# Moving operands stored from the last column to the first, and the two parts of each weight stored as a pair

## The chip, the cores and the metric

The kernel runs on one core of a Trainium2 chip. The metric is the time on the device in microseconds (us), and a time of a kernel is the median of its runs. Five engines are named throughout: PE is TensorE (matrix products; PEld is its loading of weights, which it lists apart), DVE is VectorE, ACT is ScalarE, POOL is GpSimd, and SP is SyncE, which here only issues transfers from memory.

## The reference, cut to what matters

A decoder trunk of two layers works on 272 tokens (16 learned ones and 256 real ones) of 2048 numbers each, all in float32. Layer 0 is a short gated convolution, layer 1 is attention with a forget gate over shared keys and values; each is followed by a SwiGLU with 5632 hidden units.

```python
h = concatenate([meta, x])                                    # 272 tokens x 2048
h = h + short_conv_mixer(rms_norm(h, a_norm), a_w_in, a_conv, a_w_out)
h = h + swiglu(rms_norm(h, ffn_norm[0]), ffn_w_gu[0], ffn_w_down[0])
k, v, c = shared_kv(h, kv_norm, w_kv, k_norm, w_f, b_f)       # 16 heads of 128
h = h + forgetting_attention(rms_norm(h, b_norm), b_w_q, b_q_norm, b_w_o, k, v, c)
h = h + swiglu(rms_norm(h, ffn_norm[1]), ffn_w_gu[1], ffn_w_down[1])
return h[:, 16:, :]

def swiglu(xn, w_gu, w_down):
    g, u = split(xn @ w_gu, 2, axis=-1)
    return (silu(g) * u) @ w_down
```

Nearly all of the arithmetic is products of a weight matrix with the normed tokens, and every weight (415 MB in all) is used once for each token.

## The kernel before

**How a product is made.** Activations lie transposed, 128 model dimensions on the partitions and the tokens along the free axis. A product of weights w and tokens x is made from a high and a low part of each (tiles of type fp32r): w_high x_high + w_high x_low + w_low x_high. `mm3` (lines 105 to 108) issues these three matmuls for one 128x128 block of weights, each over all tokens: 272 columns, or 256 where only the real tokens count. In layer 1's SwiGLU the two parts of x, 256 columns each, lie side by side and fit one accumulator, so that `product` (lines 110 to 121) takes both in a single matmul of 512 columns (L118 for the first, L121 for the others) and w_low x_high in one of 256 (L119). PE takes the block of weights in a load of its own (PEld) ahead of each matmul; x is the moving operand that streams past it. There are 17,126 PE instructions in the program besides loads.

**The stream of weights.** `add_panel` (line 66) cuts all weights into panels of 1 MB. SP loads them one after the other into three buffers (`RAW_BUFS`, lines 76 to 87). Each panel is two half panels, which `split` (lines 89 to 103) divides: ScalarE copies a half panel of 128 partitions x 1024 weights into the high part `whi` (L99), VectorE subtracts it from the weights and writes the low part `wlo` (L100). There are 784 half panels and four buffers for each part (`SPLIT_BUFS`). The loop at the end of the kernel (lines 774 to 781) emits the matmuls of half panel i, then the split of half panel i+3, then the steps due after i (`post` and `hooks`: gates, norms, residual adds, attention). `add_up4`, `add_up` and `add_down` (lines 123 to 204) say which blocks of weights meet which tiles of x and into which accumulator: a half panel is 24 matmuls of `mm3`, or 16 of `product`.

**The moving operands.** They are of three kinds. `make_operand` (line 231) makes the 16 tiles `x0` to `x15` of a normed input: one tile of 544 columns with the high part first and the low part behind it (L237 and L238). `put_hidden` (line 282) does the same for the tiles of the second product of a stage, in `hid` (L285, L286). `make_xb` (line 425) makes the input of the query product, in two tiles `bh` and `bl`.

**What sets the order.** The kernel is written in Tile's framework, which inserts the semaphores and sets the order of each engine's queue by a simulated timeline. Within a queue an engine works strictly in that order.

Of the kernel before, what the change touches and what calls it, by code (L numbers as in the profile page):

```python
# [10 lines left out]
F32R = mybir.dt.float32r  # L11
# [4 lines left out]
P = 128  # L16
NM = 16            # meta tokens
S = 256            # real tokens
T = NM + S         # all tokens
D = 2048  # L20
KT = D // P        # 16 tiles of the model dimension
F = 5632
FT = F // P        # 44 tiles of the hidden dimension
H = 16             # heads, each of 128
EPS = 1e-6
# [4 lines left out]

RAW_BUFS = 3       # weight panels in flight, 1 MB each
SPLIT_BUFS = 4     # half panels split into high and low parts


@with_exitstack
def kernel(ctx, tc, x, meta, a_norm, a_w_in, a_conv, a_w_out, kv_norm, w_kv,
# [15 lines left out]
    def nm(s):  # L52
        uid[0] += 1
        return f"{s}_{uid[0]}"
# [7 lines left out]

    # ---------------------------------------------------------------- weight stream
    panels, slabs, hooks = [], [], {}

    def add_panel(src, cut, mms, posts):
        """src: [128, a, b] view of 2048 elements a partition in DRAM; cut: a or b is halved."""
        j = len(panels)
        panels.append((src, cut))
        for s in range(2):  # L70
            slabs.append({"panel": j, "half": s, "mm": mms[s], "post": list(posts[s])})
        return len(slabs) - 2
# [16 lines left out]
    def split(i):  # L89
        if i >= len(slabs):  # L90
            return
        sl = slabs[i]
        j, s = sl["panel"], sl["half"]
        src, cut = panels[j]
        raw = raw_t[j].rearrange("p (a b) -> p a b", a=src.shape[1])
        part = raw[:, 4 * s:4 * s + 4, :] if cut == "a" else raw[:, :, 256 * s:256 * s + 256]
        hi = wpool.tile([P, 4, 256], F32R, tag="whi", name=nm("whi"), bufs=SPLIT_BUFS)
        lo = wpool.tile([P, 4, 256], F32R, tag="wlo", name=nm("wlo"), bufs=SPLIT_BUFS)
        A.activation(hi, part, AF.Copy)  # L99
        V.tensor_tensor(out=lo, in0=part, in1=hi.bitcast(F32), op=ALU.subtract)  # L100
        split_t[i] = (hi, lo)
        if s == 1:
            load(j + RAW_BUFS)

# [5 lines left out]
    def product(acc, cols, whi, wlo, x, first, last):  # L110
        """acc (+)= w^T x from the parts of both. With x's parts side by side the high part of w
        meets both in one instruction, and acc then holds two halves that add up."""
        xhi, xlo, both = x
        if both is None:
            mm3(acc[:, cols], whi, wlo, xhi, xlo, first, last)
        else:
            if first:
                PE.matmul(acc, whi, both, start=True, stop=False)  # L118
            PE.matmul(acc[:, S:2 * S], wlo, xhi, start=False, stop=False)  # L119
            if not first:  # L120
                PE.matmul(acc, whi, both, start=False, stop=last)  # L121

    def add_up4(w, col, xs, cols, post, delay=0):
        """Four output tiles w[:, col:col+512]^T x over all of the model dimension."""
        accs = {}
        for pnl in range(4):
            src = w[pnl * 512:(pnl + 1) * 512, col:col + 512].rearrange("(k p) c -> p k c", p=P)

            def mk(s, pnl=pnl):
                def mm(hi, lo):  # L130
                    xl = xs()
                    for m in range(2):
                        if pnl == 0:
                            accs[2 * s + m] = ps("acc")
                        for k in range(4):
                            product(accs[2 * s + m], cols, hi[:, k, m * P:(m + 1) * P],
                                    lo[:, k, m * P:(m + 1) * P], xl[4 * pnl + k],
                                    pnl == 0 and k == 0, pnl == 3 and k == 3)
                return mm

            i = add_panel(src, "b", [mk(0), mk(1)], [[], []])
        for s in range(2):
            done = lambda s=s: [post(m, accs[m]) for m in (2 * s, 2 * s + 1)]
            if delay:
                hook(i + s + delay, done)
            else:
                slabs[i + s]["post"].append(done)

    def add_up(w, col, xs, cols, post, delay=0):
        """Two output tiles w[:, col:col+256]^T x over all of the model dimension.  # L150
        post(m, acc) consumes each one."""
        accs = []
# [28 lines left out]
    def add_down(w, row, xs, cols, post, plain=16):  # L181
        """All of the 16 output tiles, with 4 tiles of the contraction from row on."""
        first = None
# [24 lines left out]

    # ---------------------------------------------------------------- constants
    ident = const.tile([P, P], F32, name="ident")  # L210
# [16 lines left out]

    # ---------------------------------------------------------------- normed operands
    state = {}

    def make_operand(key, src, gain, cols):
        """High and low parts of src * gain, for the tensor engine."""
        k = len(state[key])
        n = cols.stop - cols.start
        both = wt(f"x{k}", [P, 2 * T], F32R)
        hi, lo = both[:, 0:n], both[:, n:2 * n]
        A.activation(hi, src, AF.Copy, scale=gain)  # L237
        V.scalar_tensor_tensor(out=lo, in0=src, scalar=gain, in1=hi.bitcast(F32),  # L238
                               op0=ALU.mult, op1=ALU.subtract)
        state[key].append((hi, lo, both[:, 0:2 * n] if 2 * n <= 512 else None))  # L240

# [13 lines left out]
    def rsqrt_dve(out, m, y2):  # L255
        """out = m ** -0.5 on VectorE: a first guess from the exponent bits, then Newton."""
        V.tensor_scalar(out=out.bitcast(I32), in0=m.bitcast(I32), scalar1=-0.5,
# [18 lines left out]
    def new_hidden():  # L276
        return wt("hid", [P, 4, 2 * T], F32R, bufs=2)

    def hidden_parts(hid, k, n):
        return hid[:, k, 0:n], hid[:, k, n:2 * n]  # L280

    def put_hidden(hid, k, src, n):
        """src split into tile k of a chunk of the contraction."""
        hi, lo = hidden_parts(hid, k, n)
# [3 lines left out]
    def hidden_view(hid, n, both=False):  # L288
        return [hidden_parts(hid, k, n) + (hid[:, k, 0:2 * n] if both else None,) for k in range(4)]

# [19 lines left out]

    # ---------------------------------------------------------------- start: x to [d, token]
    start = tc.tile_pool(name="start", bufs=1)
# [56 lines left out]

    # ---------------------------------------------------------------- short convolution  # L370
    a_in, a_out = a_w_in[0], a_w_out[0]
# [53 lines left out]
    def make_xb(m):  # L425
        if m == 0:
            state["xb"] = []
        hi = wt(f"bh{m}", [P, S], F32R)
        lo = wt(f"bl{m}", [P, S], F32R)
        t = wt("bias", [P, P + NM + T], bufs=2)[:, 0:S]  # L430
# [5 lines left out]

    # ---------------------------------------------------------------- SwiGLU
    def ffn_phase(layer, cols, after):
# [48 lines left out]

    # ---------------------------------------------------------------- attention
    cdram = dram.tile([H, T], F32, name="cdram")
# [37 lines left out]
    heads = {}  # L527
    # columns of the two query blocks side by side: the first sees 144 keys, the second all
    QW = (slice(0, P + NM), slice(P + NM, P + NM + T))

    def head_square(d, name, raw, n):
        """High and low parts of the squares, for the sum over the head's 128 rows."""
        sq = wt("sq", [P, T], bufs=3)[:, 0:n]
# [7 lines left out]
    def head_norm(d, name, gain, n, tag):  # L541
        """raw * rsqrt(mean of squares + eps) * gain, split; on every partition the sums."""
        raw, sh, sl = d[name]
# [33 lines left out]

    # The keys: block A is 0:128, block B 144:272, which the first 128 queries never see, and
    # between them 16 keys whose parts are stacked on the partitions, all three products in one.
    KA, KC, KB = slice(0, P), slice(P, P + NM), slice(P + NM, T)  # L580

    def stack3(dst, src, order):
        """Tile of [high, high, low] or [high, low, high] parts of src, 16 columns each."""
        hi, again, lo = (dst[..., c:c + NM] for c in order)
# [150 lines left out]

    # ---------------------------------------------------------------- end: back to [token, d]
    fin = {}
# [23 lines left out]

    # ---------------------------------------------------------------- emission
    start_loads()
# [47 lines left out]
```

## Time and profile before

| | |
|---|---|
| time, median of 3 runs (lowest to highest) | 2381.14 us (2380.77 to 2381.97) |
| span of the profiled execution | 2376.3 us |
| PE busy | 2368.8 us, 100%, 17,266 matmuls |
| PEld busy | 2267.5 us, 95% |
| VectorE, ScalarE, GpSimd busy | 67%, 49%, 21% |
| chain of work that ended last | 97% PE |
| read from memory | 415.70 MB, 176 GB/s |

The profile is one execution, so the rows below add up to its own span and not to the median of the runs. PE works through a queue in which matmuls overlap: one begins before the one ahead of it has left the array. The durations listed for single matmuls therefore add up to more than the span, and what a matmul costs is the distance from its start to the next one's. Two views give that: single instructions in order of time, and a table by stretches, in which a count of matmuls stands beside the length of the stretch. Where PE is busy without a gap, its rows of waits say whether another engine came too late anywhere.

### The profile page before, as it was taken

What the parts mean: (1) busy time and instruction counts of PE and PEld (TensorE: products, weight loads), DVE (VectorE), ACT (ScalarE), POOL (GpSimd) and SP (SyncE); (2) the same over time, 40 slices, a digit from 0 to 9 for tenths busy, and PEclk for the clock granted to TensorE, in tenths of its full rate; (3) what the DMA queues carried; (4) which work ended last, traced back from release to release, by engine and by line L of the source; (5) the groups of instructions that cost most, each with busy time, mean ns of one, the idle gap of its engine ahead of it and who ended that gap; (6) DMA issues with size and microseconds to landing.
All of it is one profiled execution on the core that took longest, in us unless ns stands there. A gap on an engine that the chain in (4) does not pass through costs nothing.

```text
span 2376.3 us, 42180 instructions
## 1 busy us (share of the span) xinstructions
PE 2368.8 (100%) x17266; PEld 2267.5 (95%) x17266; DVE 1600.8 (67%) x2350; ACT 1170.3 (49%) x1800; POOL 505.0 (21%) x585
## 2 busy tenths in 40 slices
PE   9999999999999999999999999999999999999999
PEld 8999999999999999999999999999888888888888
DVE  6665658566556566556688667678677677777677
ACT  5443345434334333433577565666555555555555
POOL 4110113000000000000155242423033223222234
PEclk9999999999999999999999999999999999999999
DMA  6555555555555555555555555545555555555554
GB/s 228 172 175 177 178 178 178 170 173 174 177 178 178 177 175 173 172 174 177 178 163 156 164 166 165 159 151 178 195 185 187 194 183 190 190 184 195 191 182 141
DMA packets 236674, 420.53 MB, mean 177 GB/s; under 512 B 6961, under 2 KB 59281, under 8 KB 236465
## 3 DMA queue, kind: packets, MB, share of 16 engines
q1 hardware_dynamic: 235408, 415.40, 53.1%
q8 instruction: 136, 2.23, 0.4%
q0 software_dynamic: 1072, 2.44, 0.4%
q14 instruction: 58, 0.47, 0.1%
HBM read 415.70 MB, written 2.11 MB: 176 GB/s over the span
## 4 chain that ended last, share of the span: by engine, by line
PE 97%; issue 1%; DMA 1%; DVE 0%; ACT 0%; POOL 0%; SPq 0%; POOLq 0%; ACTq 0%
PE acc L107 21%; PE acc L106 21%; PE acc L108 21%; PE acc L121 18%; PE acc L119 10%; PE acc L118 3%; DMA ck<-cdram 0%; PE aux L108 0%; PE aux L107 0%; PE aux L106 0%; DMA raw<-in_a_w_in_dram 0%; PE aux L656 0%; ACT whi L99 0%; DVE wlo L100 0%; PE aux L676 0%
## 5 line engine op out<-in xcount | busy, mean ns | idle before, releaser
L100 DVE TENSOR_TENSOR wlo<-raw,whi 128x1024 fp32r<-128x1024 f32 x784 | 1019.9, 1301 | 643.5 <-ACT whi L99 638.5
L99 ACT ACTIVATE whi<-raw 128x1024 fp32r<-128x1024 f32 x784 | 829.7, 1059 | 922.2 <-PE acc L107 708.0
L106 PE MATMUL acc<-x,whi 128*128 128x272 f32 x2688 | 778.5, 290 | 0.4 <-ACT whi L99 0.4
L108 PE MATMUL acc<-x,wlo 128*128 128x272 f32 x2688 | 775.4, 289 | 0.0
L107 PE MATMUL acc<-x,whi 128*128 128x272 f32 x2688 | 774.5, 288 | 0.0
L107 PEld LDWEIGHTS acc<-x,whi 128*128 128x128 f32 x2688 | 511.4, 190 | 0.1
L106 PEld LDWEIGHTS acc<-x,whi 128*128 128x128 f32 x2688 | 505.9, 188 | 2.0 <-ACT whi L99 0.8
L108 PEld LDWEIGHTS acc<-x,wlo 128*128 128x128 f32 x2688 | 505.2, 188 | 0.0
L121 PE MATMUL acc<-x,whi 128*128 128x512 f32 x1320 | 462.0, 391 | 0.0
L119 PE MATMUL acc<-x,wlo 128*128 128x256 f32 x1408 | 380.6, 280 | 0.0
L107 PE MATMUL acc<-hid,whi 128*128 128x272 f32 (+1 forms) x1224 | 352.0, 288 | 0.0
L108 PE MATMUL acc<-hid,wlo 128*128 128x272 f32 (+1 forms) x1224 | 351.1, 287 | 0.0
L106 PE MATMUL acc<-hid,whi 128*128 128x272 f32 (+1 forms) x1224 | 349.1, 286 | 0.0
L121 PEld LDWEIGHTS acc<-x,whi 128*128 128x128 f32 x1320 | 247.8, 188 | 51.0
L119 PEld LDWEIGHTS acc<-x,wlo 128*128 128x128 f32 x1408 | 264.4, 188 | 7.4
L108 PEld LDWEIGHTS acc<-hid,wlo 128*128 128x128 f32 x1224 | 230.8, 189 | 0.1
L106 PEld LDWEIGHTS acc<-hid,whi 128*128 128x128 f32 x1224 | 230.8, 189 | 0.0
L107 PEld LDWEIGHTS acc<-hid,whi 128*128 128x128 f32 x1224 | 230.6, 188 | 0.0
L459 POOL TENSOR_TENSOR cs<-cs,rstd 128x272 f32<-128x272 f32 (+1 forms) x44 | 33.3, 756 | 911.4 <-DVE cs L457 911.4
L306 POOL TENSOR_TENSOR h<-h,u 128x256 f32<-128x256 f32 x172 | 155.6, 931 | 258.8 <-DVE h L305 258.8
L121 PE MATMUL acc<-hid,whi 128*128 128x512 f32 x522 | 192.2, 398 | 0.0
L119 PE MATMUL acc<-hid,wlo 128*128 128x256 f32 x696 | 167.2, 280 | 0.0
(194 smaller groups left out, 2378.1 us busy)
## 6 DMA issues: line engine op xcount, KB each, us to landing
raw<-in_ffn_w_gu_dram SPq DMA_DIRECT2D x176, 1024.0 KB, 5.0
raw<-in_ffn_w_down_dram SPq DMA_DIRECT2D x88, 1024.0 KB, 5.0
raw<-in_a_w_in_dram SPq DMA_DIRECT2D x47, 1024.0 KB, 5.1
raw<-in_w_kv_dram SPq DMA_DIRECT2D x32, 1024.0 KB, 5.5
raw<-in_a_w_out_dram SPq DMA_DIRECT2D x16, 1024.0 KB, 5.0
raw<-in_b_w_q_dram SPq DMA_DIRECT2D x16, 1024.0 KB, 5.3
raw<-in_b_w_o_dram SPq DMA_DIRECT2D x16, 1024.0 KB, 5.0
ck<-cdram POOLq DMA_DIRECT2D x16, 136.0 KB, 4.8
```

The source lines that it names most:

```text
L99: A.activation(hi, part, AF.Copy)
L100: V.tensor_tensor(out=lo, in0=part, in1=hi.bitcast(F32), op=ALU.subtract)
L106: PE.matmul(acc, whi, xhi, start=first, stop=False)
L107: PE.matmul(acc, whi, xlo, start=False, stop=False)
L108: PE.matmul(acc, wlo, xhi, start=False, stop=last)
L118: PE.matmul(acc, whi, both, start=True, stop=False)
L119: PE.matmul(acc[:, S:2 * S], wlo, xhi, start=False, stop=False)
L121: PE.matmul(acc, whi, both, start=False, stop=last)
L306: G.tensor_tensor(out=h[m][:, REAL], in0=h[m][:, REAL], in1=t, op=ALU.add)
L459: G.tensor_tensor(out=a, in0=a, in1=r, op=ALU.mult)
```

## The change

**The weights.** A half panel's two parts now share one tile `w2` of [128, 4, 256, 2] in place of two tiles of [128, 4, 256]: beside each high part lies its own low part. ScalarE writes every other element and VectorE reads and writes every other element; the 128x128 blocks that PE loads run over every other element too. The space is the same.

**The moving operands.** `make_operand`, `put_hidden` and `make_xb` write their tiles through a view that runs backwards, and PE reads through the same view: the first column of the operand lies at the highest address and the last at the lowest. For the joint operand of layer 1 the high part lies behind the low part, both backwards. The results in the accumulators stand in the same order as before. Operands inside attention (keys, queries, values, probabilities) stay as they were.

The rest of the diff takes out comments and docstrings, which shifts some names' numbers but no work. Every engine's queue has as many instructions of each kind as before.

```diff
@@ split
-        hi = wpool.tile([P, 4, 256], F32R, tag="whi", name=nm("whi"), bufs=SPLIT_BUFS)
-        lo = wpool.tile([P, 4, 256], F32R, tag="wlo", name=nm("wlo"), bufs=SPLIT_BUFS)
+        w2 = wpool.tile([P, 4, 256, 2], F32R, tag="w2", name=nm("w2"), bufs=SPLIT_BUFS)
+        hi, lo = w2[:, :, :, 0], w2[:, :, :, 1]
         A.activation(hi, part, AF.Copy)
         V.tensor_tensor(out=lo, in0=part, in1=hi.bitcast(F32), op=ALU.subtract)
         split_t[i] = (hi, lo)
@@ make_operand
-        both = wt(f"x{k}", [P, 2 * T], F32R)
+        both = wt(f"x{k}", [P, 2 * T], F32R)[:, 0:2 * n][:, ::-1]
         hi, lo = both[:, 0:n], both[:, n:2 * n]
         A.activation(hi, src, AF.Copy, scale=gain)
         V.scalar_tensor_tensor(out=lo, in0=src, scalar=gain, in1=hi.bitcast(F32),
                                op0=ALU.mult, op1=ALU.subtract)
-        state[key].append((hi, lo, both[:, 0:2 * n] if 2 * n <= 512 else None))
+        state[key].append((hi, lo, both if 2 * n <= 512 else None))
@@ hidden operands
+    def hidden_both(hid, k, n):
+        return hid[:, k, 0:2 * n][:, ::-1]
+
     def hidden_parts(hid, k, n):
-        return hid[:, k, 0:n], hid[:, k, n:2 * n]
+        both = hidden_both(hid, k, n)
+        return both[:, 0:n], both[:, n:2 * n]
...
     def hidden_view(hid, n, both=False):
-        return [hidden_parts(hid, k, n) + (hid[:, k, 0:2 * n] if both else None,) for k in range(4)]
+        return [hidden_parts(hid, k, n) + (hidden_both(hid, k, n) if both else None,) for k in range(4)]
@@ make_xb
-        hi = wt(f"bh{m}", [P, S], F32R)
-        lo = wt(f"bl{m}", [P, S], F32R)
+        hi = wt(f"bh{m}", [P, S], F32R)[:, ::-1]
+        lo = wt(f"bl{m}", [P, S], F32R)[:, ::-1]
```

Two places show what the scheduler makes of it. The first is ScalarE's queue in layer 0's SwiGLU: L99 is the split's copy (`whi` before, `w` after), and L455, which is L460 in the changed file, is the tanh of the gate, a step due after a half panel. Before:

```order
L455 ACTIVATE tmpb_6128<-tmpa_6126 128x272
L99 ACTIVATE whi_6164<-raw_6008 128x1024
L455 ACTIVATE tmpb_6135<-tmpa_6133 128x272
L99 ACTIVATE whi_6208<-raw_6008 128x1024
L455 ACTIVATE tmpb_6170<-tmpa_6168 128x272
L455 ACTIVATE tmpb_6177<-tmpa_6175 128x272
L99 ACTIVATE whi_6240<-raw_6066 128x1024
```

After:

```order
L460 ACTIVATE tmpb_5950<-tmpa_5948 128x272
L99 ACTIVATE w_635_5986<-raw_5834 128x1024
L460 ACTIVATE tmpb_5957<-tmpa_5955 128x272
L460 ACTIVATE tmpb_5991<-tmpa_5989 128x272
L99 ACTIVATE w_644_6029<-raw_5834 128x1024
L460 ACTIVATE tmpb_5998<-tmpa_5996 128x272
L99 ACTIVATE w_648_6060<-raw_5890 128x1024
```

The third tanh has moved from behind the second split of the panel to a place ahead of it; the rest stands as it did.

The second place is PE's queue where one half panel ends and the next begins, in the same SwiGLU, with the semaphores that PE waits for in brackets (`Activation_49` is ScalarE's, `DVE_49` VectorE's). Before:

```order
L108 MATMUL acc_6976<-x_613_4598,wlo_7080 128x272
L106 MATMUL acc_6995<-x_603_4547,whi_7107 128x272 [waits Activation_49]
L107 MATMUL acc_6995<-x_603_4547,whi_7107 128x272
L108 MATMUL acc_6995<-x_603_4547,wlo_7108 128x272 [waits DVE_49]
L106 MATMUL acc_6995<-x_605_4554,whi_7107 128x272
```

After:

```order
L108 MATMUL acc_6773<-x_482_4467,w_728_6873 128x272
L106 MATMUL acc_6791<-x_473_4417,w_729_6900 128x272 [waits Activation_49]
L107 MATMUL acc_6791<-x_473_4417,w_729_6900 128x272
L108 MATMUL acc_6791<-x_473_4417,w_729_6900 128x272 [waits DVE_49]
L106 MATMUL acc_6791<-x_475_4424,w_729_6900 128x272
```

Nothing has moved: the first matmul on a half panel waits for ScalarE, the first on its low part for VectorE, though both parts now lie in one tile.

## Rows read from the trace of the kernel before

**Rows 1.** The page: busy time by engine, and the chain that ended last

```profile
PE 2368.8 (100%) x17266; PEld 2267.5 (95%) x17266; DVE 1600.8 (67%) x2350; ACT 1170.3 (49%) x1800; POOL 505.0 (21%) x585
...
PE 97%; issue 1%; DMA 1%; DVE 0%; ACT 0%; POOL 0%; SPq 0%; POOLq 0%; ACTq 0%
```

**Rows 2.** Waits: engine, line, waited for: us in total, times, longest

```profile
ACT whi L99 <- PE acc L107: 708.0, 402, 3.6
DVE wlo L100 <- ACT whi L99: 638.5, 600, 2.1
...
PE aux L334 <- DMA growa<-in_a_norm_dram: 1.3, 1, 1.3
```

**Rows 3.** Four stages: convolution, SwiGLU 0, attention, SwiGLU 1; columns stand first

```profile
core 0: us, PE busy (x) PEld busy (x) DVE busy (x) ACT busy (x) POOL busy (x), PEclk, DMA share, GB/s
60.00:490.00 430.00, 430.00 (x3429) 429.92 (x3428) 271.86 (x350) 180.82 (x219) 62.64 (x68) 1.00 0.53 175
490.00:1010.00 520.00, 520.00 (x4152) 520.00 (x4151) 308.63 (x408) 203.46 (x233) 21.93 (x28) 1.00 0.53 175
1010.00:1560.00 550.00, 549.28 (x4437) 543.99 (x4436) 387.86 (x692) 314.81 (x579) 170.61 (x207) 1.00 0.52 167
1640.00:2330.00 690.00, 690.00 (x3959) 605.17 (x3958) 498.37 (x670) 365.97 (x573) 176.65 (x190) 1.00 0.57 190
```

**Rows 4.** Single starts in order of time: start us, us, engine, line, operation

```profile
599.72 0.29 PE L106 MATMUL acc<-x,whi 128*128 128x272 f32 x1
599.85 0.29 PE L107 MATMUL acc<-x,whi 128*128 128x272 f32 x1
599.85 0.19 PEld L108 LDWEIGHTS acc<-x,wlo 128*128 128x128 f32 x1
...
605.88 0.29 PE L107 MATMUL acc<-x,whi 128*128 128x272 f32 x1
...
1613.87 0.28 PE L107 MATMUL acc<-hid,whi 128*128 128x256 f32 x1
...
1616.96 0.28 PE L107 MATMUL acc<-hid,whi 128*128 128x256 f32 x1
...
1661.74 0.40 PE L121 MATMUL acc<-x,whi 128*128 128x512 f32 x1
...
1662.09 0.39 PE L121 MATMUL acc<-x,whi 128*128 128x512 f32 x1
...
1669.79 0.39 PE L121 MATMUL acc<-x,whi 128*128 128x512 f32 x1
...
1771.71 0.39 PE L121 MATMUL acc<-x,whi 128*128 128x512 f32 x1
...
1779.95 0.39 PE L121 MATMUL acc<-x,whi 128*128 128x512 f32 x1
```

**Rows 5.** The splits (min/median/max ns), VectorE's in SwiGLU 1

```profile
L99 ACT ACTIVATE whi<-raw x784: 1042/1062/1095, 8.9 to 2358.9; 128x1024 fp32r<-128x1024 f32 x196
...
L100 DVE TENSOR_TENSOR wlo<-raw,whi x784: 1208/1225/3064, 10.0 to 2360.0; 128x1024 fp32r<-128x1024 f32 x196
...
1640.00:2330.00 690.00, 330.43 (x249) 1.00 0.57 190
```

**Rows 6.** Three transposes with their weight loads, in order of time

```profile
1300.25 0.49 PE L656 MATMUL aux<-ident,sc 128*128 128x128 f32 x3
...
L656 PE MATMUL aux<-ident,sc 128*128 128x128 f32 x48 | 8.2, 280 | 0.0
```

**Rows 7.** The page's groups of matmuls: shape, xcount, busy us, mean ns of one

```profile
L106 PE MATMUL acc<-x,whi 128*128 128x272 f32 x2688 | 778.5, 290 | 0.4 <-ACT whi L99 0.4
...
L119 PE MATMUL acc<-x,wlo 128*128 128x256 f32 x1408 | 380.6, 280 | 0.0
...
L106 PE MATMUL acc<-hid,whi 128*128 128x272 f32 (+1 forms) x1224 | 349.1, 286 | 0.0
...
L119 PE MATMUL acc<-hid,wlo 128*128 128x256 f32 x696 | 167.2, 280 | 0.0
```

## The prediction

> **What bounds the kernel now.** [...] Then PE's own waits: six entries, none above 1.3 us, against 708.0 us that ScalarE and 638.5 us that VectorE stand idle before a split [rows 2]. So nothing feeds PE too late; the time is the number of matmuls times their spacing. A matmul's listed duration (about 290 ns) overlaps its neighbours', so the spacing must be read from starts or counts. Stretch by stretch, the count over the time gives 520.00 us / 4152 = 125.2 ns in layer 0's SwiGLU and 690.00 / 3959 = 174.3 ns in layer 1's, where 512 and 256 columns alternate [rows 3]. From single starts: 49 steps of 272 columns take 6.16 us, 125.7 ns each; 26 steps of 256 columns take 3.09 us, 118.8 ns; a pair of 512 and 256 takes 343.3 ns in one stretch (24 pairs in 8.24 us) and 350.0 ns in another of the same loop (23 in 8.05 us) [rows 4].
>
> These four give a slope and a fixed part. Sixteen columns more cost 6.9 ns, 0.43 a column; 256 columns more, 343.3 or 350.0 less two times 118.8, cost 0.41 to 0.44. With 0.42 ns a column, what is left per matmul is 11.5 ns (272), 11.3 (256), 10.3 or 13.7 (half a pair). **About 11.5 ns on each of some 17,000 matmuls, 196 us or 8% of the span, is not streaming of columns.** Each matmul has its own weight load, which starts as the matmul before it starts (599.85 for the load and the matmul ahead) [rows 4]. The two stretches of 512 and 256 run the same instructions on the same shapes and differ by 2%; in the slower one the 512s alternate between 0.39 and 0.40 us with the tile of x, in the faster one they don't [rows 4]. So the fixed part is not quite fixed: it moves with how the operands lie and how their two reads fall together. That is what this change touches.
>
> **The change part by part.** No instruction is added or removed: the five queues hold the same counts as before. Four things change.
>
> *Order.* The scheduler moves 36 of ScalarE's 922 other instructions and 76 of VectorE's 1504 one place ahead of a split, five of each one place behind; GpSimd's stand as before against its residual adds, SP's queue is the same, and on PE some 50 matmuls, most of them in attention, stand a few places elsewhere. In layer 0's SwiGLU a post step goes ahead of a split, so that split starts later by its time, less than a split's own 1.06 us [rows 5]. Its cover is the idle time before it: 708.0 us over 402 waits, 1.8 us each [rows 2], and PE is three half panels behind, 24 matmuls or 3.0 us each. On VectorE the same move is covered by its 638.5 us of idle time. SP's next load waits for VectorE's read of the panel, and its own first split stands five half panels, 15 us, further on; the one load among PE's waits is at the start. Cost: zero.
>
> *One tile for both parts.* A matmul on the high part still waits for ScalarE alone and the first on the low part for VectorE. A slot comes free for ScalarE when its last matmul of either part is done, at most one matmul (0.13 us) later than now, against 1.8 us of slack: zero.
>
> *Writers.* The 784 splits now write every other element (ScalarE 1062 ns, VectorE 1225 ns in the median), and VectorE also reads so; the makers of x and hid write backwards [rows 5]. No row has such a step, so I bound it by these instructions' own rows: 1208 ns, the shortest, and 3064, the longest [rows 5]. I take no change; PE would notice only above the point given under the second rival. The start, where L106 waits 0.4 us for its first split [rows 7], adds that split's growth, 2 us at most.
>
> [...]
>
> *PE's two reads.* The moving operand runs down through memory while the weights run up, at twice the step. The prices lie between two ends. If the fixed part went entirely: 17,000 x 11.5 ns = 196 us less. If it doubled: 196 us more. Between the rows that are there, 10.3 and 13.7 ns, lies the spread of one and the same layout, -20 to +37 us. I take a gain, of **half the fixed part**, 17,000 x 5.75 ns = 98 us: the alternating stretch shows two reads that keep meeting in step when both run upwards, and reads that run against each other pass once and don't stay in step. That is argued, not shown; half is the middle between nothing and all of it.
>
> **Sum.** Profiled span 2376.3 less 98 (reads), and 0 for order, tile and writers: 2278 us. The runs' median, 2381.14, is 4.8 us above the span; so **2283 us**.
>
> **The rivals.**
>
> *No change.* The fixed part may be the array's own, say the exchange of weights, and not care where operands lie. For it: it is 11.5 and 11.3 ns for 272 and 256 columns although these stretches read different tiles. Against it: the two stretches of one loop. Time 2376 to 2386. [...]
>
> *First rival on the other side: weights at every other element load slower.* The place is the load that runs beside each matmul. Three transposes of 128 columns, each with its own load, take 0.49 us from the first start to the last end, and one alone 0.28: 0.105 us apart, which bounds the load now [rows 6]. It hides under 118.8 or 125.7 ns. So the point from which it decides is a load 13% longer for 256 columns, 20% for 272. At 0.131 us: 3 x (2688 + 1224) = 11,736 matmuls of L106 to L108, nearly all of 272 columns, x 5.5 ns, and 2104 of L119 x 12.4 ns [rows 7]: +91 us, 2472. At twice, 0.21 us: 11,736 x 84.5 + 2104 x 91 ns = +1183 us: 3564. For it: the slack is small. Against it: nothing shows the load near a limit of memory.
>
> *Second: strided writing makes VectorE the bound.* The tightest stage is layer 1's SwiGLU: 498.4 us busy of 690, with 249 splits [rows 3, 5], so a split may grow by 0.77 us, from 1.33 to 2.10, before VectorE decides. At twice the median, 2.45 us: 498 + 249 x 1.12 = 778 of 690 us, +88 us in this stage alone: 2470 or more. ScalarE, at 49%, could double and still be hidden.
>
> *Third: the reads meet more often.* Twice as many weight bytes are passed over per load. With the slow row's 13.7 ns everywhere: +37 us, 2418; with the fixed part doubled: 2577.
>
> **How the numbers follow.** Gain from the reads 0.55 (2185 to 2376); no change 0.13; weights load slower 0.10 (2400 to 3564); VectorE the bound 0.09 (2390 to 2500); reads meet more often 0.13 (2390 to 2577). About 0.2%, 5 us, is what a measurement of this kernel can tell from no change, and the alternatives on PE are all larger than that. Faster 0.55, same 0.13, slower 0.32. For the range I leave out 0.03 of the gain below 2205 (where under 1.2 ns of the fixed part would be left) and 0.17 of the slow cases above 2450: the slower loads above a load of about 0.12 us, half of the two others. That is 2205 to 2450; the likeliest case alone is 2205 to 2376.
>
> **What would show it.** Right: stretches as in rows 3 with the same 100% PE and counts, but shorter, layer 0's SwiGLU near 119.5 ns a matmul and layer 1's near 168.5; PE without waits; splits within a few per cent of 1062 and 1225 ns. Half right: spacing falls for one shape only. No change: 125.2 and 174.3 again. Slow loads: spacings of 256 and 272 columns become equal, while 512s keep theirs. VectorE the bound: PE waits for L100 by name, and VectorE near 100% in layer 1. The prediction is wrong in its main step if the spacing doesn't fall, whatever else happens.

## The result and the profile after

The changed kernel takes **2395.43 us** (median; 2394.16 to 2397.99), the kernel before 2380.95 beside it: a ratio of **1.0065**, 95% interval 1.0053 to 1.0077. It is 14.5 us slower, where 98 us of gain were forecast.

The page of the profiled execution: its span, busy time by engine, and the chain that ended last, as in [rows 1]:

```profile
span 2396.2 us, 42035 instructions
...
PE 2386.7 (100%) x17266; PEld 2294.6 (96%) x17266; DVE 1582.3 (66%) x2350; ACT 1260.1 (53%) x1800; POOL 513.6 (21%) x585
...
PE 98%; DMA 1%; POOL 0%; ACT 0%; DVE 0%; issue 0%; SPq 0%; POOLq 0%; ACTq 0%
```

PE has the same number of matmuls as before and is busy all the time, as before, only for longer. The first four lines below are all that it waits for (engine, line, what was waited for: us in total, times, longest); the last two stand beside [rows 2]:

```profile
PE aux L339 <- DMA growa<-in_a_norm_dram: 1.2, 1, 1.2
PE warm L224 <- POOL epsb L217: 1.1, 1, 1.1
PE aux L663 <- DVE c L592: 1.1, 1, 1.1
PE aux L347 <- DMA m<-in_meta_dram: 0.5, 1, 0.5
...
ACT w L99 <- PE acc L108: 664.1, 414, 3.7
DVE w L100 <- ACT w L99: 699.0, 580, 2.3
```

No split is among PE's waits, and ScalarE and VectorE still stand idle ahead of theirs. The splits themselves, as in [rows 5] (minimum/median/maximum in ns):

```profile
L99 ACT ACTIVATE w<-raw x784: 1111/1182/1242, 8.6 to 2377.0; 128x1024 fp32r<-128x1024 f32 x196
...
L100 DVE TENSOR_TENSOR w<-raw,w x784: 1189/1227/2941, 9.8 to 2378.2; 128x1024 fp32r<-128x1024 f32 x196
```

ScalarE pays 120 ns for writing every other element (1062 before), VectorE 2 ns (1225). Neither reaches PE. The loss is in the spacing of the matmuls, in the same stretches as [rows 3] (the columns are named there):

```profile
60.00:490.00 430.00, 430.00 (x3409) 429.93 (x3408) 269.41 (x349) 197.43 (x218) 63.10 (x68) 1.00 0.52 174
490.00:1010.00 520.00, 520.00 (x4131) 520.00 (x4130) 300.03 (x399) 224.82 (x230) 28.83 (x28) 1.00 0.51 175
1010.00:1560.00 550.00, 548.89 (x4398) 543.63 (x4398) 380.63 (x680) 326.14 (x564) 172.11 (x201) 1.00 0.51 165
1640.00:2330.00 690.00, 690.00 (x3925) 614.54 (x3925) 490.58 (x667) 389.51 (x570) 179.20 (x194) 1.00 0.54 188
```

Each stretch holds fewer matmuls in the same time at the same granted clock (1.00): 520 us / 4131 = 125.9 ns in layer 0's SwiGLU (125.2 before), 690 / 3925 = 175.8 in layer 1's (174.3).

**Where the loss is.** The trace has the start of every matmul to the nanosecond, so the distance from each start to the next can be averaged by line, by tile of x and by the address that the program gives the tile. "Three products" is the distance from an L106 to the next one, on a tile of x with 272 columns (2688 of them in the kernel; the few behind which another kind of matmul or a wait comes are left out of the mean). Even and odd tiles are x0, x2, ... and x1, x3, ...:

| ns from start to start | before | after | difference x count |
|---|---|---|---|
| three products, even tiles of x | 380.3 | 374.1 | |
| three products, odd tiles of x | 372.5 | 385.5 | |
| three products, mean | 376.4 | 379.8 | 3.4 x 2688 = +9.1 us |
| L121 on x, 512 columns | 228.9 | 235.3 | 6.4 x 1320 = +8.4 us |
| L119 on x, 256 columns | 118.0 | 118.0 | 0 |
| the same operations on hid | | | -3.2 us |

With +1.7 us for the products of 256 columns in attention and +0.4 for L118, that is 16 to 17 us. The two profiled executions differ by 19.9 us (2376.3 and 2396.2), the medians of the runs by 14.5; most of the rest lies behind the last product with weights (1.7 us) and in PE's transposes and the products inside attention (1.5 us). The view of single starts shows the mean of the third row over four tiles, 601.93 - 600.41 = 1.52 us, 380 ns each:

```profile
600.41 0.29 PE L106 MATMUL acc<-x,w 128*128 128x272 f32 x1
...
601.93 0.29 PE L106 MATMUL acc<-x,w 128*128 128x272 f32 x1
```

That row is a mean over two very different ones: before the change the even tiles were the slow ones, after it the odd ones are, by more. Nothing that the matmuls do tells them apart but where they lie. A tile of x is 2176 bytes, which is 128 more than a multiple of 256; so even tiles begin at 96 modulo 256 and odd ones at 224, before and after.

### The profile page after: what moved, and what is told of

It reads as the page before. It is cut to its first block, busy times and chain, and to the rows that moved or that the text cites. A ratio compares the mean times of both kernels' runs of the same rounds, so it can differ in the third digit from the quotient of the medians.

```text
span 2396.2 us, 42035 instructions
## 1 busy us (share of the span) xinstructions
PE 2386.7 (100%) x17266; PEld 2294.6 (96%) x17266; DVE 1582.3 (66%) x2350; ACT 1260.1 (53%) x1800; POOL 513.6 (21%) x585
## 4 chain that ended last, share of the span: by engine, by line
PE 98%; DMA 1%; POOL 0%; ACT 0%; DVE 0%; issue 0%; SPq 0%; POOLq 0%; ACTq 0%
PE acc L106 22%; PE acc L108 21%; PE acc L107 21%; PE acc L121 18%; PE acc L119 10%; PE acc L118 3%; PE aux L106 0%; PE aux L107 0%; PE aux L108 0%; PE aux L349 0%; PE aux L661 0%; DMA ck<-cdram 0%; PE aux L681 0%; DMA m<-in_meta_dram 0%; DVE w L100 0%
## 5 line engine op out<-in xcount | busy, mean ns | idle before, releaser
L100 DVE TENSOR_TENSOR w<-raw,w 128x1024 fp32r<-128x1024 f32 x784 | 1003.1, 1280 | 704.9 <-ACT w L99 699.0
L99 ACT ACTIVATE w<-raw 128x1024 fp32r<-128x1024 f32 x784 | 927.8, 1184 | 847.8 <-PE acc L108 664.1
L106 PE MATMUL acc<-x,w 128*128 128x272 f32 x2688 | 790.8, 294 | 0.0
L107 PE MATMUL acc<-x,w 128*128 128x272 f32 x2688 | 783.1, 291 | 0.0
L108 PE MATMUL acc<-x,w 128*128 128x272 f32 x2688 | 778.9, 290 | 0.0
L108 PEld LDWEIGHTS acc<-x,w 128*128 128x128 f32 x2688 | 535.0, 199 | 0.1
L106 PEld LDWEIGHTS acc<-x,w 128*128 128x128 f32 x2688 | 526.3, 196 | 1.4 <-ACT w L99 0.3
L107 PEld LDWEIGHTS acc<-x,w 128*128 128x128 f32 x2688 | 527.3, 196 | 0.1
L121 PE MATMUL acc<-x,w 128*128 128x512 f32 x1320 | 470.2, 398 | 0.0
L119 PE MATMUL acc<-x,w 128*128 128x256 f32 x1408 | 383.4, 283 | 0.0
L106 PE MATMUL acc<-hid,w 128*128 128x272 f32 (+1 forms) x1224 | 351.1, 288 | 0.0
L107 PE MATMUL acc<-hid,w 128*128 128x272 f32 (+1 forms) x1224 | 351.0, 287 | 0.0
L108 PE MATMUL acc<-hid,w 128*128 128x272 f32 (+1 forms) x1224 | 350.2, 286 | 0.0
L121 PEld LDWEIGHTS acc<-x,w 128*128 128x128 f32 x1320 | 256.9, 195 | 47.5
L119 PEld LDWEIGHTS acc<-x,w 128*128 128x128 f32 x1408 | 275.1, 195 | 7.1
L107 PEld LDWEIGHTS acc<-hid,w 128*128 128x128 f32 x1224 | 237.6, 194 | 0.0
L108 PEld LDWEIGHTS acc<-hid,w 128*128 128x128 f32 x1224 | 237.5, 194 | 0.0
L106 PEld LDWEIGHTS acc<-hid,w 128*128 128x128 f32 x1224 | 236.9, 194 | 0.2
L121 PE MATMUL acc<-hid,w 128*128 128x512 f32 x522 | 191.1, 397 | 0.0
L119 PE MATMUL acc<-hid,w 128*128 128x256 f32 x696 | 167.2, 281 | 0.0
```

The source lines that it names most:

```text
L106: PE.matmul(acc, whi, xhi, start=first, stop=False)
L107: PE.matmul(acc, whi, xlo, start=False, stop=False)
L108: PE.matmul(acc, wlo, xhi, start=False, stop=last)
```

## The experiments

Three theories. **Direction**: an operand that is read backwards costs. **Pairs**: a load of every other weight costs. **Places**: neither costs by itself, and the spacing follows from where the addresses of the reads stand, modulo some small power of two.

### The two halves of the change apart

The first run is the changed kernel with two tiles for the parts of the weights again:

```diff
-        w2 = wpool.tile([P, 4, 256, 2], F32R, tag="w2", name=nm("w2"), bufs=SPLIT_BUFS)
-        hi, lo = w2[:, :, :, 0], w2[:, :, :, 1]
+        hi = wpool.tile([P, 4, 256], F32R, tag="whi", name=nm("whi"), bufs=SPLIT_BUFS)
+        lo = wpool.tile([P, 4, 256], F32R, tag="wlo", name=nm("wlo"), bufs=SPLIT_BUFS)
```

> The changed kernel with its moving operands backwards, but the high and low parts of the weights in two tiles again. Theory 'direction' (a moving operand read downwards costs): 2395 us like the changed kernel, L107 of 272 columns 127.4 ns from start to start and L121 of 512 columns 234.8. Theory 'pairs' (the load of every other weight costs): 2381 us like the kernel before, L107 125.4 and L121 231.0. Theory 'places' (neither costs by itself; the spacing follows from where the two read addresses stand to each other): a time of its own, and the two halves of the change do not add up to its 14.5 us.

Measured: 2390.64 us, ratio 1.0049 (1.0036 to 1.0062); over x and hid together L107 took 125.1 ns, near what "pairs" wanted (125.4), and L121 235.8, near what "direction" wanted (234.8). The second run is the kernel before with the opposite edit.

> The kernel before with the high and low parts as pairs in one tile; moving operands forwards. 'Direction': 2381 us, spacings as before (L106, L107, L108 of 272 columns 126.3, 125.4, 125.8 ns, L121 231.0). 'Pairs': 2395 us, 127.6, 127.4, 124.7 and 234.8. 'Places': a time of its own, not 14.5 us less the effect of the reversal. ScalarE's split 1184 ns (1059 before) whatever theory holds, without a wait of PE.

Measured: 2397.84 us, ratio 1.0077 (1.0064 to 1.0090); L106, L107 and L108 at 127.4, 125.8 and 126.3 ns and L121 at 235.0, over x and hid together, so L106 and L121 near "pairs" and the other two near "direction". ScalarE's split took 1146 ns in the mean, not the 1184 that was expected whatever holds. Layer 0's SwiGLU and layer 1's, backwards alone and then pairs alone:

```profile
490.00:1010.00 520.00, 520.00 (x4133) 520.00 (x4132) 306.41 (x402) 201.88 (x231) 21.79 (x28) 1.00 0.51 175
1640.00:2330.00 690.00, 690.00 (x3919) 598.87 (x3918) 489.83 (x662) 362.14 (x567) 176.93 (x193) 1.00 0.55 188
```

```profile
490.00:1010.00 520.00, 520.00 (x4130) 520.00 (x4130) 300.50 (x400) 219.10 (x231) 28.80 (x28) 1.00 0.51 174
1640.00:2330.00 690.00, 690.00 (x3933) 616.79 (x3932) 493.94 (x669) 383.60 (x570) 177.23 (x194) 1.00 0.55 188
```

Either half alone costs about what both cost together (0.5% and 0.8%, against 0.65%), in both layers. Two causes that each cost something by itself would add up to 1.3%. Neither "direction" nor "pairs" can be the account by itself. The halves don't even lose where the whole does. With both, the three products on x lose most (376.4 to 379.8 ns); with either half alone they hardly move (376.7 backwards, 377.4 in pairs), and it is L121 on x (228.9 to 236.4 and to 234.8) and the three products on hid (375.0 to 379.9 and to 380.0, where both together take 373.3) that are slower.

The third run has both parts in one tile, but as two blocks:

```diff
+        w2 = wpool.tile([P, 2, 4, 256], F32R, tag="w2", name=nm("w2"), bufs=SPLIT_BUFS)
+        hi, lo = w2[:, 0], w2[:, 1]
```

> The kernel before with both parts in one tile, but as two blocks of 1024 columns, one behind the other: what one tile, its semaphores and the scheduler's order do by themselves. All theories: within 0.2% of 2381 us; ScalarE's split 1059 ns. If it is slower by 14 us, the cost is in the tile or the order and not in the reads.

Measured: 2379.37 us, ratio 0.9997 (0.9988 to 1.0006); ScalarE's split 1058 ns in the mean, L121 on x 228.9. One tile, its semaphores and the order that follows from it cost nothing.

### Moving the operands by a few bytes

The next run is the changed kernel with 8 unused columns (32 bytes) at the end of each tile of x:

```diff
-        both = wt(f"x{k}", [P, 2 * T], F32R)[:, 0:2 * n][:, ::-1]
+        both = wt(f"x{k}", [P, 2 * T + 8], F32R)[:, 0:2 * n][:, ::-1]
```

> The changed kernel with 32 bytes more between one tile of x and the next, so that the 16 tiles begin at 8 different places modulo 256 bytes (in the changed kernel they begin at two, 96 and 224). 'Places': the spacing of the three products of 272 columns takes more levels than the 374 and 386 ns for three that the two kinds of tiles show in the changed kernel, each set by the tile's place; tiles at 192 as low as the 372 to 375 ns of the hidden operand, which begins there. 'Direction' and 'pairs': all tiles near the mean of 380, no order by place; time 2395 us.

Measured: 2380.99 us, ratio 1.0005 (0.9996 to 1.0015). The three products take 371 to 382 ns, depending on where the tile begins, 374.9 in the mean. Thirty-two unused bytes a tile give the whole loss back, with every operand still backwards and every weight still in a pair. Tiles that begin at 192, where hid begins, take 372.9, within what was expected there. One thing did not fit a tile's own place as the cause: one tile with two different tiles ahead of it differs (L107 on x8: 125.0 ns behind x11, 127.5 behind x7).

The same pad in the kernel before:

> The kernel before with 32 bytes more between one tile of x and the next, so that they begin at 8 places modulo 256 bytes in place of 2. 'Places': again several levels, each tied to a place, and L121 no longer in the two even paths of 224 and 230 to 235 ns; the time moves by some us either way, 2375 to 2395. 'Direction' and 'pairs' (now with their sum not holding): nothing here is backwards or in pairs, so 2381 and one level of 376 ns for three products.

Measured: 2381.82 us, ratio 1.0006 (0.9997 to 1.0015): three products 375.2 in place of 376.4, L121 232.0 in place of 228.9. The levels are there, the gain and the loss cancel.

Next, the changed kernel with the weights' tiles 128 bytes further up and x and hid 512 bytes up, which is their old place modulo 512:

```diff
-    warm = const.tile([P, 1], F32, name="warm")
+    warm = const.tile([P, 33], F32, name="warm")
...
+        ahead = 96 if k == 0 else 0
+        both = wt(f"x{k}", [P, ahead + 2 * T], F32R)[:, ahead:ahead + 2 * n][:, ::-1]
```

> The changed kernel with the tiles of the weights 128 bytes further up and all of x and hid at their old places modulo 512. 'Places' in the form that the distance between moving operand and weights counts: even and odd tiles of x trade their spacings: L106 from 129.0 and 125.8 ns (starts at 92 and 220) to 125.8 and 129.0, L107 from 130.7 and 125.0 (28 and 156) to 125.0 and 130.7. If only the places of the moving operand count (one moving operand against the next): no change. Time 2390 to 2400 by both.

Measured: 2394.68 us, ratio 1.0064 (1.0048 to 1.0079). The tiles of x trade places to a tenth of a nanosecond: L106 125.8 where it was 129.0 and 129.0 where it was 125.8; L107 125.0 and 130.6; three products 385.6 on even tiles and 374.1 on odd ones, where it was 374.1 and 385.5. Of what these products read, only the weights moved (modulo 512), so what counts has the address of the weights in it. Layer 0's SwiGLU, in which the mean is all that is seen, is the same to the matmul:

```profile
490.00:1010.00 520.00, 520.00 (x4131) 520.00 (x4131) 299.77 (x401) 225.22 (x231) 28.67 (x28) 1.00 0.51 175
```

Then x moved by 96 bytes in both kernels, so that its tiles begin where hid's begin modulo 256; the weights stay, and hid stays modulo 512. In the changed kernel:

```diff
-        both = wt(f"x{k}", [P, 2 * T], F32R)[:, 0:2 * n][:, ::-1]
+        ahead, behind = (24 if k == 0 else 0), (104 if k == KT - 1 else 0)
+        both = wt(f"x{k}", [P, ahead + 2 * T + behind], F32R)[:, ahead:ahead + 2 * n][:, ::-1]
```

> The changed kernel with all tiles of x 96 bytes further up, so that they begin where the tiles of hid begin modulo 256 bytes; hid stays. 'Places': three products of x take hid's 371.6 and 375.0 ns by turns in place of 374.1 and 385.5, 6.5 less in the mean x 2688 = 17.5 us; L121 hid's 233.5 in place of 235.3, 2.4 us; L119 0.9 ns x 1408, 1.3 us: 2374 us, faster than the kernel before by 0.3%. 'Direction' or 'pairs': 2395.

Measured: **2373.93 us, ratio 0.9973 (0.9963 to 0.9983)**: three products 373.4, L121 233.3, L119 116.8. This is the lowest median of the case, 7 us under the kernel before and 21 us under the changed one, by 96 bytes.

> The kernel before with the same shift of x. By its own hid rows: 375.0 ns for three products in place of 376.4, 3.8 us less; L121 236 in place of 229, 9 us more; L119 1 us less: 2385 us. So 'places' wants the same shift to help the changed kernel and to help this one not at all; a shift that helped both would point to something in the tiles of x themselves.

Measured: 2383.38 us, ratio 1.0015 (1.0007 to 1.0024); three products 375.2, L121 233.7. The shift that takes 21 us from the changed kernel adds 2 or 3 to the one before, as its own rows on hid had said. The two stretches, of the changed kernel moved and of the kernel before moved:

```profile
490.00:1010.00 520.00, 520.00 (x4181) 520.00 (x4180) 306.97 (x414) 229.11 (x235) 28.66 (x28) 1.00 0.52 177
1640.00:2330.00 690.00, 690.00 (x3945) 614.44 (x3944) 489.61 (x665) 391.24 (x576) 180.62 (x194) 1.00 0.55 189
```

```profile
490.00:1010.00 520.00, 520.00 (x4163) 520.00 (x4162) 310.10 (x409) 203.99 (x234) 21.85 (x28) 1.00 0.52 177
1640.00:2330.00 690.00, 690.00 (x3918) 602.01 (x3917) 490.62 (x660) 361.10 (x564) 164.48 (x188) 1.00 0.55 188
```

### All tiles at one place

Four runs give every tile of x the same place modulo 256 by a pad of 32 columns, for which one of three buffers of the squares is given up; the place is set by the columns ahead of x0:

```diff
-        both = wt(f"x{k}", [P, 2 * T], F32R)[:, 0:2 * n][:, ::-1]
+        ahead, behind = (24 if k == 0 else 0), {11: 48, KT - 1: 8}.get(k, 32)
+        both = wt(f"x{k}", [P, ahead + 2 * T + behind], F32R)[:, ahead:ahead + 2 * n][:, ::-1]
...
-            t = wt("sq", [P, T], bufs=3)
+            t = wt("sq", [P, T], bufs=2)
```

> The changed kernel with all 16 tiles of x at one place modulo 256 bytes, the better of hid's two (high part starts at 188): 371.6 ns for three products in every tile, where the shift by 96 bytes had 371.8 and 375.0 by turns: 1.7 x 2688 = 4 us less, 2370 us, if a tile's spacing doesn't depend on the place of the tile after it; 2374 or more if it does. One of the three buffers of the squares is given up for the space; PE should not wait for that.

> The kernel before with the same places (high part at 192 or 448 modulo 512). By its own hid rows 374.3 ns for three products at 192 and 367.5 at 448, 370.9 in the mean in place of 376.4: 5.5 x 2688 = 15 us less; L121 231 in place of 229, 3 us more: 2369 us, if hid's rows carry over; about 2381 if the spacing hangs on the order of places too.

> The changed kernel with all tiles of x at its worse place (high part starts at 92, low part at 28): a dose of the suspected cost. Three products 385.5 ns in every tile in place of 374.1 and 385.5 by turns: 5.7 x 2688 = 15 us more, L121 237.5 in place of 235.4, 3 us more: 2413 us. Without the theory of places: 2395.

The expectations of the first and the third name the wrong places. Read backwards, a high part of n columns starts 8n - 4 bytes behind the start of the tile; in a tile at 192 that is 60 for n = 272 and 188 for the joint operand of 512 columns (n = 256), at 96 it is 220 and 92. So the third run put x, for 272 columns, where the even tiles lie in the changed kernel and not at the costly place. The last run does that.

> The changed kernel with all tiles of x at 224 modulo 256 bytes, where the odd tiles lie in it: a high part of 272 columns starts at 92, a low part at 28, the joint operand of 512 columns at 220. (The run with all tiles at 96 moved them to the place of the even ones, 220 and 156 for 272 columns, not to the place that its expectation names.) If a tile's own place sets its spacing: three products 385.5 ns in every tile in place of 379.8 in the mean, 15 us more, L121 233.3 in place of 235.3, 3 us less, 2407 us. If it is the step from the place of the tile ahead to its own (in the run with tiles 32 bytes apart a tile's spacings differ with the tile ahead of it, L107 125.0 or 127.4 ns), the loss goes with the alternation, and this is near the 2374 to 2380 us of the other runs with a single place.

| tiles of x begin at (modulo 256) | us | ratio (interval) | three products, even / odd | L121 |
|---|---|---|---|---|
| after: 96 and 224 by turns | 2395.43 | 1.0065 (1.0053 to 1.0077) | 374.1 / 385.5 | 235.3 |
| after, moved: 192 and 64 by turns | 2373.93 | 0.9973 (0.9963 to 0.9983) | 375.0 / 371.8 | 233.3 |
| after, all at 192 | 2375.48 | 0.9980 (0.9970 to 0.9989) | 373.4 / 373.4 | 233.9 |
| after, all at 96 | 2379.10 | 0.9997 (0.9987 to 1.0006) | 373.4 / 373.4 | 235.9 |
| after, all at 224 | 2376.27 | 0.9984 (0.9975 to 0.9994) | 373.5 / 373.5 | 232.5 |
| before: 96 and 224 by turns | 2380.95 | 1 | 380.3 / 372.5 | 228.9 |
| before, all at 192 | 2375.98 | 0.9985 (0.9975 to 0.9994) | 373.6 / 373.5 | 232.2 |

The first expectation's 2370 us missed (2375.48; "2374 or more" if the next tile's place counts was right), and the second's two values, 2369 and 2381, lie on either side of 2375.98.

Layer 0's SwiGLU with all tiles at 192, 96 and 224 in the changed kernel:

```profile
490.00:1010.00 520.00, 520.00 (x4181) 520.00 (x4180) 307.07 (x414) 228.99 (x235) 28.65 (x28) 1.00 0.53 177
```

```profile
490.00:1010.00 520.00, 520.00 (x4181) 520.00 (x4180) 306.64 (x413) 227.51 (x234) 28.67 (x28) 1.00 0.53 177
```

```profile
490.00:1010.00 520.00, 520.00 (x4181) 520.00 (x4180) 306.64 (x413) 230.53 (x234) 28.61 (x28) 1.00 0.52 177
```

Three runs with x at three places hold the same 4181 matmuls in 520 us, the changed kernel 4131. The starts, here with all tiles at 224, show the same: four tiles take 601.60 - 600.11 = 1.49 us, 373 ns each, where it was 1.52.

```profile
600.11 0.29 PE L106 MATMUL acc<-x,w 128*128 128x272 f32 x1
...
601.60 0.29 PE L106 MATMUL acc<-x,w 128*128 128x272 f32 x1
```

Even at 224, where the odd tiles of the changed kernel take 385.5 ns, the three products take 373.5 once the tile ahead lies at the same place. So a tile's own place is not the cause either, and 2407 us was wrong. In each of these runs the tiles lie at two places modulo 512 and at one modulo 256, so a place that agrees modulo 256 was enough for 373.4 to 373.6 ns. The loss on the three products is there only where places alternate, and not at every pair of places: in the changed kernel a step of 128 bytes between high parts that start at 60 and 188 (x moved by 96 bytes) costs nothing in the mean, between 92 and 220 it costs 11 to 12 ns on every other tile, and which tile pays goes with the address of the weights. Giving up a buffer of the squares cost nothing that shows: no wait of PE in these runs is longer than 1.9 us, and none is for a split beyond 0.3. And forwards with weights apart, at one place, it is 373.5 as well: **with the tiles at one place the direction and the pairs together make no difference to the three products** (neither half was run there alone). L121, which is nearly half of the loss, follows no rule that these runs show: at one place it takes 232.2 ns forwards and 232.5 to 235.9 backwards and in pairs, and the kernel before, where it goes through stretches of 224 and of 230 to 235 by turns, has the lowest mean of all layouts, 228.9 (also with the two parts as blocks in one tile). That is why its single place gained it less than the changed kernel's.

Why a step between 92 and 220 costs with the weights at 96 modulo 256 and one between 60 and 188 does not is open. So is why it takes the pairs as well: backwards alone the starts are the same 92 and 220, with high and low parts of the weights all at 96, and the three products took 377.0 ns on even tiles and 376.4 on odd ones. The runs show which layouts clash, not what in the chip they clash on.

## Why the prediction was wrong, point by point

**What bounds the kernel: right.** PE's spacing sets the time before and after, in every stretch. PE's waits are 3.7 us in total before (five lines, not the six that the prediction counted) and 3.9 us after.

**Order, one tile, writers at nothing: right.** The run with two blocks in one tile gave 0.9997, and PE waits for no split in the changed kernel. ScalarE's writes cost 120 ns each (1182 in the median against 1062), 784 x 120 ns = 94 us over the kernel, and none of it reaches PE: ScalarE still stands idle for 664.1 us before a split, waiting for L108, and for 183.6 us waiting for L121. VectorE's split, which now reads one input and writes its output at every other element, took 1227 ns in the median against 1225; the second rival, which needed a growth of 0.77 us, fell with that.

**The weights don't load slower as far as the time goes: the first rival fell.** L119 on x stayed at 118.0 ns from start to start, where a load that decides would have shown first. The loads do get longer: their listed time is 194 to 196 ns in the mean in every run with pairs and 188 to 189 in every run without. But it goes with the pairs and not with the time of the kernel: 194.2 in the kernel of 2373.93 us, 188.5 in the one that is backwards alone (2390.64 us).

**PE's two reads: the step that failed.** "I take a gain, of half the fixed part" rested on the author's picture that two upward reads keep meeting in step and two opposed ones pass once; no row or run shows it. Backwards alone the kernel became slower by 0.5%, and at one place both directions take 373.4 to 373.6 ns. The observation under it was right: the fixed part isn't quite fixed and moves with how the operands lie. What it moves by was mis-sized. In all 14 kernels the three products on x took 373.4 to 379.9 ns in the mean, which is 124.5 to 126.6 for one matmul; a gain of 5.75 ns was taken, and 1.0 less to 1.2 more than before is what there is. Layer 0's SwiGLU went from 125.2 ns a matmul to 125.9, and layer 1's from 174.3 to 175.8, where 119.5 and 168.5 were the sign of being right. The rest of the fixed part, an estimated 10 ns (124.5 less 272 x 0.42), is in every layout. The text had the right bound in hand: the spread of one and the same layout, 10.3 to 13.7 ns, "-20 to +37 us". The measured +14.5, and the -7 of the best layout, lie in it; the value taken lay outside, between ends for which no row spoke. That 2395 us lies between 2205 and 2450 is no credit to the sum: the slow rivals had widened the range that far.

**The third rival is the one that came out**, the reads that meet more often: +37 us at the slow row's 13.7 ns everywhere was its lower price, 14.5 was measured. Only its outcome is shown. Its reason, the bytes that a load of pairs passes over, is not: contiguous weights lost as well once the operands ran backwards (ratio 1.0049), and pairs lost nothing with all tiles at one place (0.9980 to 0.9997). It was given 0.13.

**Against the rival of no change** the 2% between the two stretches of layer 1 were rightly held up. The run in which the weights moved by 128 bytes, and even and odd tiles traded 374.1 and 385.5 ns, bears them out: there too the same instructions on the same shapes took another time at another place.

## What to carry to other kernels

Where PE is busy without a gap, compare starts of like matmuls tile by tile before explaining a mean: two levels that follow a tile's address (374.1 and 385.5 ns here) can be a matter of places, and a pad of a few columns on the operand tests it, as here, where 96 bytes were worth more (21 us) than the whole change (14.5 us). When a layout is changed and the time moves by half a per cent, undo it half by half and then move the result by a few bytes, because the new layout may have been judged by one unlucky place. And a term that no row shows is sized by the spread that the rows do show, not by the middle of what could be imagined.

## What the runs showed of the hardware

- In the changed kernel the spacing of matmuls goes with addresses modulo 256 bytes: grouped by the places of a matmul's and the next one's moving operand and weights, L106 to L108 of 272 columns scatter by 0.6 ns about their group's mean (2.5 ns ungrouped; 1.9 grouped modulo 128, and 0.6 again modulo 512). It is not the whole account: over the seven layouts that are backwards and in pairs the same grouping leaves 1.0 ns of 2.0, and in the kernel before 1.3 of 2.3.
- Moving the weights by 128 bytes, with the moving operands at their old places modulo 512, exchanges the spacings of even and odd tiles (374.1 and 385.5 ns became 385.6 and 374.1), so where the weights lie enters the spacing.
- The place of the tile ahead counts: three products take 373.4 to 373.6 ns at any single place that was tried (three), and 370.9 to 385.6 on even or odd tiles where two places alternate.
- ScalarE's copy of 1024 elements to every other place takes 1182 ns in the median against 1062; VectorE's subtraction with one such read and such writes 1227 against 1225.
- A load of 128x128 weights at every other place is listed with 194 to 196 ns in place of 188 to 189; L119 on x, of 256 columns, takes 118.0 ns from start to start in the kernel before and in the changed one alike.
